# Row chains of a two-layer trunk: the norm weight's product beside the sum of squares, one operation behind the root; the second down projection's last rows, and the last store, by column halves

## Chip, cores and metric

The kernel runs on one core of one Trainium2 chip. The metric is the device time of one execution in microseconds (us), the median of several runs. The engines named below are PE (TensorE, matrix products), ACT (ScalarE), DVE (VectorE), POOL (GpSimd) and SP (SyncE, which here only issues loads). Each engine works through its own list of instructions in order; a value made on one engine is waited for on another by a semaphore. DMAs are issued by SP (loads) and by ACT (stores and a few loads).

## The reference

1024 rows of 1024 numbers pass two layers. In each, a mixer (layer 0: a gated short convolution, layer 1: attention with low-rank queries, keys and values) and an MLP with a squared ReLU (inner width 4096) work on the normalised rows, and their result is normalised again, weighted and added to the stream:

```python
def rmsnorm(x, g):
    xf = x.astype(jnp.float32)
    y = xf * lax.rsqrt(jnp.mean(xf * xf, axis=-1, keepdims=True) + NORM_EPS)
    return (y * g.astype(jnp.float32)).astype(x.dtype)
...
        x = x + g_m[:, None, :] * rmsnorm(y, norm_g[l, 1])
        h = modulate(rmsnorm(x, norm_g[l, 2]), sh_f, sc_f)
        y = squared_relu_mlp(h, mlp_up_w[l], mlp_down_w[l])
        x = x + g_f[:, None, :] * rmsnorm(y, norm_g[l, 3])
    return x
```

The two lines `x = x + g * rmsnorm(y, ...)`, four in all, are the row chains that the change touches. The conditioning `g` and the norm weight are one row of 1024 numbers, held in all 128 partitions as `gmb`; the root's factor differs from row to row.

## The kernel before

**Products.** Each fp32 operand is split into a high part, which ACT copies, and a low part, which DVE subtracts (`split_w`, L158). A product is three matmuls of 128x512 (`mm`, L154): low by high, high by low, high by high. The MLPs work in column and row halves with seven products in place of eight (`first_pairs`, `down_pairs`).

**Row chain.** The rows stand in eight tiles `ys[t]` of 128x1024. `Seam.tile` (L318) does for tile t: `add()`, which adds the last part of the product from PSUM to `y` (DVE, L829 of `down` with 1024 columns or L694 of `down_pairs` with 512); `back()`, the DVE half of steps begun earlier; the squares of `y` with their row sum and the root on ACT (L271, L273); `flush()` of the tile before; for t >= 5 two `front` steps; the reciprocal (L278) and y times root times `gmb` in one operation (L327, DVE); the sum with the stream's rows `xr` (L328, DVE); the store of `xr` to DRAM, issued by ACT (L329); the squares and root of `xr`. `flush` (L311) scales `xr` by its own root into `y`, which is then ready to be turned.

**Steps.** The next product needs the rows turned: its operands have the 1024 columns in partitions. Step k (eight for each half of four tiles) turns four 128x128 blocks on PE (L373, L433) and scales and shifts them on ACT (L374, L436); that is its `front`. Its `back` is the split on DVE: L384/L385 in `first_pairs`' operands, and the low part L442 alone where ACT writes the high part itself.

**The four seams.** Two are at the end of `down` (convolution's output, attention's output): for each of eight tiles 24 matmuls go into one of two PSUM tiles `big`, and `seam.tile` follows. The eight steps of the first half are done between tiles 5 to 7 and in `first_pairs` behind them. There `first(0)`, `first(1)`, `second(0)` are the first products; after `second(0)` a fourth block of weights, `late` (L594, an `ad` tile with the tag "acc", one buffer), is split. The other two seams are those of `down_pairs`: tiles 0 to 3 are finished while it still multiplies, tiles 4 to 7 in the loop at its end, 24 matmuls each. In layer 0 the first half's steps run in that loop, and behind it come `first_latents` (L571: three row blocks m, each over k = 0 to 7, so that block m = 0 needs step k's high part and then its low part) and, in block m = 2, the second half's steps, which need tile 7's `flush`. In layer 1 nothing comes behind: the store of tile 7 to the output is the end.

**Order.** `pinned()` keeps the order in which the program is written on all engines but SP; elsewhere, and on SP, a scheduler orders by priority and by when buffers come free. `down_pairs` loads the rows `xr` of tiles 0 to 5 ahead (`early`), by turns into a tile with the tag "xr" and into the "acc" tile.

## Time and profile before

| | us |
|---|---|
| median of 3 runs | 2160.37 (2159.45 to 2161.99) |
| the profiled execution | 2159.2 |
| its span, first to last instruction or transfer | 2157.4 |
| PE busy | 2062.0 (96%) |
| DVE busy | 1541.2 (71%) |
| ACT busy | 1084.3 (50%) |
| first seam: adds of tiles 0 to 7 (L829) | 345.9 to 388.8 |
| second seam's last four tiles: adds (L694) | 1019.1 to 1039.4 |
| third seam: adds (L829) | 1469.1 to 1513.2 |
| last seam's last four tiles: adds (L694) | 2132.3 to 2149.3 |

The granted clock of PE is a mean of 0.991 over the span. In a timeline a row has the start, the duration, the engine, the line, the operation, what it writes and reads with shapes, how many instructions were joined, and in brackets the idle time ahead and what ended it. A row of waits has the total, the number and the longest of the waits of one line for another.

### The profile page before, as it was taken

To read this page: it belongs to the slowest core of one execution; us is meant where nothing else is said; L and a number is where in the kernel's file an instruction comes from. 1 tells how busy PE (TensorE), PEld (TensorE's weight loads), DVE (VectorE), ACT (ScalarE), POOL (GpSimd) and SP (SyncE) were. 2 spreads that over 40 slices of the span, in tenths; PEclk is the share of its full clock that TensorE was granted. 3 is DMA by queue.
4 is the path that set the end of the run, shared out by engine and by line. 5 is a ranking of instruction groups with operands and counts; after the bars stand their busy time and mean duration, and the time that the engine had idled before them with its cause. 6 is when DMAs were issued, how large, how long until landed. Compare 5 with 4: busy or idle time off the path is not lost.

```text
span 2157.4 us, 25064 instructions
## 1 busy us (share of the span) xinstructions
PE 2062.0 (96%) x9438; PEld 1688.2 (78%) x9438; DVE 1541.2 (71%) x2087; ACT 1084.3 (50%) x1533; POOL 5.3 (0%) x13
## 2 busy tenths in 40 slices
PE   4999999989999999999899999999899999999998
PEld 3788878768888788888677788887678888788886
DVE  6877876876665669977688887756875665566576
ACT  4533353745554444455665565555744444544443
POOL 0000000000000000000000000000000000000000
PEclk9999999999999999999999999999999999999999
DMA  7444464254553889656223331143254653774355
GB/s 223 121 138 147 137 205 133 88 184 161 182 181 139 280 292 322 208 166 211 69 70 120 97 96 35 59 135 138 71 185 150 215 180 134 266 252 158 98 175 167
DMA packets 251023, 344.47 MB, mean 160 GB/s; under 512 B 19253, under 2 KB 142482, under 8 KB 250902
## 3 DMA queue, kind: packets, MB, share of 16 engines
q1 hardware_dynamic: 208408, 252.50, 37.4%
q10 hardware_dynamic: 42494, 90.38, 11.3%
q8 instruction: 74, 1.21, 0.2%
q14 instruction: 47, 0.39, 0.1%
HBM read 258.94 MB, written 83.89 MB: 159 GB/s over the span
## 4 chain that ended last, share of the span: by engine, by line
PE 77%; DVE 11%; ACT 6%; DMA 3%; issue 2%; ACTq 0%; SPq 0%; DVEq 0%
PE one L156 42%; PE mm L156 20%; PE tp L156 7%; PE big L156 3%; PE big L1360 2%; ACT junk L271 2%; DVE y L327 1%; PE tp L1386 1%; DVE raw L328 1%; DMA aw<-in_ada_w_dram 1%; ACT slot L1210 1%; DVE av L909 1%; PE tp L433 1%; DVE ring L160 1%; DVE acc L186 1%
## 5 line engine op out<-in xcount | busy, mean ns | idle before, releaser
L156 PE MATMUL one<-slot,uphi 128*128 128x512 f32 x1224 | 377.8, 389 | 0.0
L156 PEld LDWEIGHTS one<-slot,uphi 128*128 128x128 f32 x1224 | 230.4, 188 | 48.3 <-issue 0.5
L156 PE MATMUL one<-ring,ring 128*128 128x512 f32 x1152 | 262.9, 389 | 2.3 <-DVE ring L160 2.3
L160 DVE TENSOR_TENSOR uplo<-raw,uphi 128x1024 fp32r<-128x1024 f32 x127 | 153.3, 1222 | 143.1 <-ACT uphi L159 143.1
L156 PEld LDWEIGHTS one<-ring,ring 128*128 128x128 f32 x1152 | 215.9, 188 | 48.3 <-ACT ring L159 3.1
L156 PE MATMUL one<-slot,uplo 128*128 128x512 f32 x612 | 240.7, 393 | 8.2 <-DVE y L528 3.8
L160 DVE TENSOR_TENSOR ring<-raw,ring 128x1024 fp32r<-128x1024 f32 x144 | 174.3, 1220 | 55.6 <-ACT ring L159 55.3
L159 ACT ACTIVATE ring<-raw 128x1024 fp32r<-128x1024 f32 x144 | 149.5, 1052 | 106.6 <-DMA raw<-ha 61.6
L159 ACT ACTIVATE uphi<-raw 128x1024 fp32r<-128x1024 f32 x127 | 134.7, 1061 | 118.6 <-PE one L156 82.3
L156 PE MATMUL mm<-ring,ring 128*128 128x512 f32 x768 | 185.0, 390 | 1.6 <-DVE ring L160 1.6
L156 PE MATMUL tp<-ring,ring 128*128 128x512 f32 x768 | 183.9, 389 | 0.0
L159 ACT ACTIVATE ring<-w 128x1024 fp32r<-128x1024 f32 x80 | 84.8, 1060 | 178.7 <-PE tp L156 102.7
L156 PEld LDWEIGHTS mm<-ring,ring 128*128 128x128 f32 x768 | 143.7, 188 | 32.1 <-DVE ring L160 2.5
L156 PEld LDWEIGHTS tp<-ring,ring 128*128 128x128 f32 x768 | 144.1, 188 | 29.9
L160 DVE TENSOR_TENSOR ring<-w,ring 128x1024 fp32r<-128x1024 f32 x80 | 97.8, 1222 | 81.1 <-ACT ring L159 81.1
L156 PEld LDWEIGHTS one<-slot,uplo 128*128 128x128 f32 x612 | 115.2, 188 | 35.8 <-DVE y L528 5.5
L186 DVE SCALAR_TENSOR_TENSOR acc<-raw,csil,acc 128x1024 f32<-128x1024 f32 x88 | 112.5, 1278 | 22.8 <-DMA raw<-in_ada_w_dram 18.0
L526 ACT ACTIVATE y<-one 128x512 f32<-128x512 f32 x66 | 39.0, 591 | 159.6 <-PE one L156 118.5
L156 PE MATMUL mm<-slot,uphi 128*128 128x512 f32 x344 | 109.2, 399 | 9.6 <-DVE slot L398 9.4
L156 PE MATMUL one<-slot,s 128*128 128x512 f32 x468 | 112.9, 390 | 1.1 <-DVE s L160 1.1
L156 PEld LDWEIGHTS one<-slot,s 128*128 128x128 f32 x468 | 87.6, 188 | 20.6 <-DVE s L160 2.4
L156 PE MATMUL one<-q,uphi 128*128 128x512 f32 x328 | 101.9, 392 | 0.0
(267 smaller groups left out, 3614.4 us busy)
## 6 DMA issues: line engine op xcount, KB each, us to landing
ha<-y ACTq DMA_DIRECT2D x224, 256.0 KB, 4.0
raw<-ha SPq DMA_DIRECT2D x112, 512.0 KB, 4.0
raw<-in_ada_w_dram SPq DMA_DIRECT2D x80, 512.0 KB, 4.3
raw<-in_mlp_up_w_dram SPq DMA_DIRECT2D x70, 512.0 KB, 4.5
w<-in_mlp_down_w_dram SPq DMA_DIRECT2D x48, 512.0 KB, 7.0
raw<-in_mlp_down_w_dram SPq DMA_DIRECT2D x32, 512.0 KB, 4.0
raw<-in_conv_in_w_dram SPq DMA_DIRECT2D x18, 512.0 KB, 4.1
xs<-raw ACTq DMA_DIRECT2D x18, 512.0 KB, 2.8
```

Of the source, the lines that this page charges most:

```text
L156: nc.tensor.matmul(out_, lhs[a], rhs[b], start=first and i == 0, stop=last and i == 2, skip_group_check=more)
L159: nc.scalar.activation(hi, src, AF.Copy)
L160: nc.vector.tensor_tensor(lo, src, hi.bitcast(F32), op=ALU.subtract)
L186: nc.vector.scalar_tensor_tensor(acc, raw, s, acc, op0=ALU.mult, op1=ALU.add)
L271: nc.scalar.activation(junk, src, AF.Square, accum_out=ss)
L327: nc.vector.scalar_tensor_tensor(y, y, rroot(ss), self.gmb, op0=ALU.mult, op1=ALU.mult)
L328: nc.vector.tensor_tensor(xr, xr, y, op=ALU.add)
L433: nc.tensor.transpose(p_[:, t * P:(t + 1) * P], ys[half * 4 + t][:, k * P:(k + 1) * P], ident)
L526: nc.scalar.activation(dst, x_, AF.Copy)
L909: nc.vector.scalar_tensor_tensor(acc, raw[:, i, :], csil[:, i:i + 1], acc, op0=ALU.mult, op1=ALU.add)
L1210: nc.scalar.activation(y[32 * i:32 * i + 32, :], p_[32 * j:32 * j + 32, :], AF.Copy, scale=scale)
L1360: nc.tensor.matmul(o_, a, m_, start=j == 0, stop=j == 4)
```

## The change

It does six things.

1. In seams 1 and 3 for all tiles, and in `down_pairs` for tiles 5 to 7 (`seam.beside`), the product with the norm weight, `yg = y * gmb`, is an operation of its own on DVE, which needs no root, into the "acc" tile. Behind the root one operation is left, `xr = yg * root + xr`.
2. The store of `xr` is issued after the squares and the root of `xr`, and `back()` stands at the end of the tile.
3. In tiles 5 to 7 of `down_pairs` (`part`) the second column half, which needs no add any more, is squared and weighted ahead of the add; only the first half's squares follow the add, with the other sum as the root's bias.
4. The last tile's last operation and its store go by column halves, the second half's store by SP.
5. Tile 5's `xr` in `down_pairs` is no longer loaded ahead into the "acc" tile.
6. `late` shares the "acc" buffer with `yg`, and so is loaded behind the last `yg`.

```diff
-    def squares(nx, src):
+    def squares(nx, src, more=None):
...
-        nc.scalar.activation(rt, ss, AF.Sqrt, bias=eps_d)
+        nc.scalar.activation(rt, ss, AF.Sqrt, bias=eps_d if more is None else more)
...
-        def tile(self, t, add, steps):
+        def tile(self, t, add, steps, held=False, part=False):
...
+            beside = add is not None and t >= self.beside
+            part = part and beside
+            yg = ad.tile([P, D], F32, tag="acc", name=nm("yg"), bufs=1) if beside else None
+
+            def gained(cols):
+                nc.vector.tensor_tensor(yg[:, cols], y[:, cols], self.gmb[:, cols], op=ALU.mult)
+
             with pinned():
+                if part:
+                    some = small()
+                    junk = self.nx.tile([P, D], BF16, tag="junk", name=nm("junk"), bufs=1)
+                    nc.scalar.activation(junk[:, HALF:], y[:, HALF:], AF.Square, accum_out=some)
+                    nc.vector.tensor_tensor(some, some, eps_d, op=ALU.add)
+                    gained(slice(HALF, D))
                 if add:
                     add()
-                self.back()
-                ss = squares(self.nx, y)
+                if beside:
+                    gained(slice(0, HALF if part else D))
+                else:
+                    self.back()
+                if part:
+                    ss = squares(self.nx, y[:, :HALF], some)
+                else:
+                    ss = squares(self.nx, y)
                 self.flush()
                 if t >= 5:
                     self.front(steps, 2)
-                nc.vector.scalar_tensor_tensor(y, y, rroot(ss), self.gmb, op0=ALU.mult, op1=ALU.mult)
-                nc.vector.tensor_tensor(xr, xr, y, op=ALU.add)
-                nc.scalar.dma_start(self.xdst[t * P:(t + 1) * P, :], xr)
+                rs = rroot(ss)
+                if not beside:
+                    nc.vector.scalar_tensor_tensor(y, y, rs, self.gmb, op0=ALU.mult, op1=ALU.mult)
+                    nc.vector.tensor_tensor(xr, xr, y, op=ALU.add)
+                elif self.last and t == NT - 1:
+                    for n, queue in enumerate((nc.scalar, nc.sync)):
+                        cols = slice(n * HALF, (n + 1) * HALF)
+                        nc.vector.scalar_tensor_tensor(xr[:, cols], yg[:, cols], rs, xr[:, cols], op0=ALU.mult, op1=ALU.add)
+                        queue.dma_start(self.xdst[t * P:(t + 1) * P, cols], xr[:, cols])
+                    return
+                else:
+                    nc.vector.scalar_tensor_tensor(xr, yg, rs, xr, op0=ALU.mult, op1=ALU.add)
                 if not self.last:
-                    self.rest = (y, xr, squares(self.nx, xr))
+                    self.rest = (y, xr, None, t) if held else (y, xr, squares(self.nx, xr), None)
+                if not held:
+                    nc.scalar.dma_start(self.xdst[t * P:(t + 1) * P, :], xr)
+                if beside:
+                    self.back()
...
-                    early(i // 2)
+                    if i < 10:
+                        early(i // 2)
...
-            seam.ahead = 4
+            seam.ahead, seam.beside = 4, 5
...
-                    seam.tile(4 + t, lambda: done(t, banks_[t]), [])
+                    seam.tile(4 + t, lambda: done(t, banks_[t]), [], False, True)
```

`held` is false everywhere. Inside `tile`, the lines after the change are 36 higher than before (L442 becomes L478, L694 becomes L730, L829 becomes L866).

First place: DVE in the first seam, around the add of tile 6 (`y_2274`; `raw_2772` and then `raw_2775` are the stream's rows of tile 5, `slot_2260` the operand that the steps fill). Before:

```order
L328 TENSOR_TENSOR raw_2772<-raw_2772,y_2273 128x1024
L829 TENSOR_TENSOR y_2274<-y_2274,big_2897 128x1024
L384 CAST slot_2260<-q_2279 128x512
L385 TENSOR_TENSOR slot_2260<-q_2279,slot_2260 128x512
L384 CAST slot_2260<-q_2280 128x512
L385 TENSOR_TENSOR slot_2260<-q_2280,slot_2260 128x512
L278 RECIPROCAL small_2932<-small_2895 128x1
L278 RECIPROCAL small_2947<-small_2930 128x1
L327 SCALAR_TENSOR_TENSOR y_2274<-y_2274,small_2947,gmb_1086 128x1024
L328 TENSOR_TENSOR raw_2818<-raw_2818,y_2274 128x1024
```

After the change, in the same place:

```order
L361 SCALAR_TENSOR_TENSOR raw_2775<-yg_2871,small_2894,raw_2775 128x1024
L420 CAST slot_2260<-q_2279 128x512
L421 TENSOR_TENSOR slot_2260<-q_2279,slot_2260 128x512
L420 CAST slot_2260<-q_2280 128x512
L421 TENSOR_TENSOR slot_2260<-q_2280,slot_2260 128x512
L866 TENSOR_TENSOR y_2274<-y_2274,big_2907 128x1024
L328 TENSOR_TENSOR yg_2932<-y_2274,gmb_1086 128x1024
L278 RECIPROCAL small_2940<-small_2900 128x1
L278 RECIPROCAL small_2955<-small_2938 128x1
L361 SCALAR_TENSOR_TENSOR raw_2822<-yg_2932,small_2955,raw_2822 128x1024
```

The four rows of the two steps moved from behind tile 6's add to ahead of it, the second of the two long rows behind the root is gone, and the product with `gmb` stands between the add and the reciprocals.

Second place: DVE in `down_pairs` of layer 0, tile 5 (`y_5371`, later `y_5379`) and the low part of step 6 (`h_1013_7203` from `tt_7536`, later `h_1021_7211` from `tt_7544`), from the end of tile 4 on. Before:

```order
L328 TENSOR_TENSOR xr_7240<-xr_7240,y_5370 128x1024
L694 TENSOR_TENSOR y_5371<-y_5371,mm_6855 128x512
L442 TENSOR_TENSOR h_1013_7203<-tt_7536,h_1012_7202 128x512
L278 RECIPROCAL small_7558<-small_7529 128x1
L278 RECIPROCAL small_7561<-small_7556 128x1
L327 SCALAR_TENSOR_TENSOR y_5371<-y_5371,small_7561,gmb_4317 128x1024
L328 TENSOR_TENSOR xr_7326<-xr_7326,y_5371 128x1024
```

After the change:

```order
L353 TENSOR_TENSOR xr_7248<-xr_7248,y_5378 128x1024
L335 TENSOR_TENSOR small_7560<-small_7560,eps_d 128x1
L328 TENSOR_TENSOR yg_7559<-y_5379,gmb_4325 128x512
L730 TENSOR_TENSOR y_5379<-y_5379,mm_6863 128x512
L328 TENSOR_TENSOR yg_7559<-y_5379,gmb_4325 128x512
L278 RECIPROCAL small_7572<-small_7536 128x1
L278 RECIPROCAL small_7575<-small_7570 128x1
L361 SCALAR_TENSOR_TENSOR raw_7517<-yg_7559,small_7575,raw_7517 128x1024
L478 TENSOR_TENSOR h_1021_7211<-tt_7544,h_1020_7210 128x512
```

The low part of step 6 moved from the row behind tile 5's add to behind its last operation, and the 128x1 sum L335, which needs ACT's squares of the second half, now stands ahead of the add. The low part of step 7 stands likewise behind tile 6's last operation. The same rows of ACT, from tile 4's root on, before:

```order
L329 DMA xs_104<-xr_7240 128x1024
L271 ACTIVATE junk_7526,small_7527<-xr_7240 128x1024
L273 ACTIVATE small_7529<-small_7527,eps_d 128x1
L436 ACTIVATE h_1012_7202<-one_7531,v_6810,v_6806 128x512
L436 ACTIVATE tt_7536<-one_7531,v_6810,v_6806 128x512
L271 ACTIVATE junk_7553,small_7554<-y_5371 128x1024
L273 ACTIVATE small_7556<-small_7554,eps_d 128x1
L311 ACTIVATE y_5370<-xr_7240,small_7558 128x1024
```

After the change:

```order
L271 ACTIVATE junk_7533,small_7534<-xr_7248 128x1024
L273 ACTIVATE small_7536<-small_7534,eps_d 128x1
L365 DMA xs_104<-xr_7248 128x1024
L472 ACTIVATE h_1020_7210<-one_7539,v_6818,v_6814 128x512
L472 ACTIVATE tt_7544<-one_7539,v_6818,v_6814 128x512
L334 ACTIVATE junk_7561,small_7560<-y_5379 128x512
L271 ACTIVATE junk_7567,small_7568<-y_5379 128x512
L273 ACTIVATE small_7570<-small_7568,small_7560 128x1
L311 ACTIVATE y_5378<-xr_7248,small_7572 128x1024
```

The whole squares of tile 5 became two of half the columns, and the first of them (L334) stands behind the store of tile 4.

Third place: SP in the first seam, between the loads of the stream's last rows and the next weights (`w_3041` is `late`, `acc_4327` a row of biases for the conditioning). After the change:

```order
L296 DMA raw_2869<-in_x_dram 128x1024
L114 DMA raw_3043<-in_mlp_up_w_dram 128x8x128
L114 DMA raw_3045<-in_mlp_up_w_dram 128x8x128
L114 DMA w_3041<-in_mlp_up_w_dram 128x8x128
L114 DMA acc_4327<-in_ada_b_dram 1x1024
L114 DMA raw_3382<-in_mlp_up_w_dram 128x8x128
```

Before, `late` stood 21 rows further up, ahead of most of the output projection's weights:

```order
L114 DMA raw_2438<-in_conv_out_w_dram 128x1024
L114 DMA raw_2442<-hd_116 128x1024
L114 DMA w_3029<-in_mlp_up_w_dram 128x8x128
L114 DMA raw_2558<-in_conv_out_w_dram 128x1024
L114 DMA raw_2562<-hd_117 128x1024
```

It moved past the loads of all eight tiles' rows, and now waits for tile 7's last operation, since it shares the buffer with `yg`. In the third seam it moved in the same way. On PE the transposes of the steps around tiles 6 and 7 of seams 1 and 3 are grouped otherwise between the matmuls; in `down_pairs` and at the end PE's order is the same.

10 lines of the change are left out of this document (6 added, 4 removed).

## The prediction

> **What bounds the kernel now.** I read the page first, for the engine that sets the pace.
>
> ```profile
> span 2157.4 us, 25064 instructions
> PE 77%; DVE 11%; ACT 6%; DMA 3%; issue 2%; ACTq 0%; SPq 0%; DVEq 0%
> ```
>
> The second line is the chain that ended last: 77% of the span is PE's own work, and DVE and ACT appear where PE stands still for them. The change touches no matmul, so it can only move the stretches in which PE waits, the matmuls that run slowly after a wait, and the tail behind the last matmul. The waits of PE come next, by who is waited for.
>
> ```profile
> PE tp L433 <- ACT y L311: 5.8, 2, 5.2
> PE tp L373 <- ACT q L374: 4.9, 4, 2.3
> ```
>
> Both belong to the seams: 4.9 us in four waits for the scaled transposes of seams 1 and 3, and 5.8 us for the normalised last rows of seam 2. The timeline of the end of seam 1 shows what these waits are made of.
>
> ```profile
> 381.50 1.22 DVE L829 TENSOR_TENSOR y<-y,big 128x1024 f32<-128x1024 f32 x1
> ...
> 383.38 1.04 ACT L271 ACTIVATE junk<-y 128x1024 bf16<-128x1024 f32 x1
> ...
> 384.55 0.30 ACT L273 ACTIVATE small<-small,eps_d 128x1 f32<-128x1 f32 x1
> ...
> 385.08 1.28 DVE L327 SCALAR_TENSOR_TENSOR y<-y,small,gmb 128x1024 f32<-128x1024 f32 x1
> ...
> 385.34 0.48 PE L156 MATMUL big<-slot,slot 128*128 128x512 f32 x1
> ...
> 386.40 1.23 DVE L328 TENSOR_TENSOR raw<-raw,y 128x1024 f32<-128x1024 f32 x1
> 386.82 1.33 PE L373 MATMUL tp<-cs,y 128*128 128x128 f32 x8 [1.01 <-ACT q L374]
> 387.54 1.21 DVE L829 TENSOR_TENSOR y<-y,big 128x1024 f32<-128x1024 f32 x1
> ...
> 390.99 1.15 ACT L311 ACTIVATE y<-raw,small 128x1024 f32<-128x1024 f32 x1
> ...
> 392.05 1.43 ACT L374 ACTIVATE q<-tp,v,v 128x512 f32<-128x512 f32 x2
> ...
> 392.86 1.78 PE L373 MATMUL tp<-cs,y 128*128 128x128 f32 x8 [1.19 <-ACT q L374]
> ...
> 401.58 1.05 ACT L159 ACTIVATE uphi<-w 128x1024 fp32r<-128x1024 f32 x1
> ```
>
> PE has finished tile 7's matmuls at 385.8, but its add (L829) starts only at 387.54: the chain lags PE. From that add on everything is serial: squares, root, L311, then the scaled transposes at 392.05, for which PE waits. The clock pays once more:
>
> ```profile
> 380.00:393.00 13.00, 10.57 (x51) 7.60 (x50) 12.69 (x20) 11.25 (x20) 0.00 (x0) 1.00 0.49 161
> 393.00:397.00 4.00, 4.00 (x15) 3.31 (x15) 2.99 (x6) 3.38 (x7) 0.00 (x0) 0.57 0.33 131
> 1048.70:1052.00 3.30, 3.30 (x11) 2.72 (x12) 1.12 (x2) 1.48 (x2) 0.00 (x0) 0.52 0.02 5
> ```
>
> The columns are the stretch, its length, busy time of PE, weight loads, DVE, ACT and POOL, the granted clock and the DMAs. In 380 to 393 DVE is busy for 12.69 of 13 us. In 393 to 397 PE gets 0.57 of its clock, so 4.0 x 0.43 = 1.7 us of its work is lost; behind the long wait of seam 2 it is 3.3 x 0.48 = 1.6 us.
>
> **The change part by part. Seam 1.** L327 and L328 behind the root (1.28 + 1.23) become one operation; I price it by L327, which has two tensors and a column too, at 1.28. The product `yg` costs as much as L328 (1.23) but runs on DVE while ACT squares (1.04 and more). So one L328 leaves the cycle: two adds of before lie 6.04 us apart (381.50 and 387.54), and 6.04 - 1.23 is 4.8. PE needs 5.44 for a tile's 24 matmuls (the adds at the very end, shown below, follow PE: 2148.64 - 2137.77 is two tiles), so PE becomes the pace, and the lag vanishes up to tile 5. For tiles 6 and 7 the steps' splits fill DVE again, as the 12.69 of 13 shows. Written out engine by engine in the new order, the queues give tile 7's add at 386.4, 1.15 earlier. Its squares start when the add ends, at 387.6; 1.4 for squares and root on ACT (383.38 to the end of 384.55's row is 1.47) and 1.06 of L311 (390.99 to 392.05) put the scaled transposes at 390.1 instead of 392.05, so **-2.0**. PE still waits there, some 1.1 us by the same sum, but the wait of 1.01 at 386.82 goes since steps 2 and 3 are turned earlier. With one short wait instead of two I take the slow stretch as gone: **-1.3** of the 1.7, since PE would lose part of it to the same chain anyway. Together -3.3, or -2.0 if the clock drops as before.
>
> The store behind the squares costs nothing: ACT had to issue it in the same cycle before. `back()` at the tile's end costs nothing in this seam, for the casts wait for ACT's L374 in either place.
>
> **Seam 3** has the same code and a worse lag:
>
> ```profile
> 1508.44 0.48 PE L156 MATMUL big<-slot,slot 128*128 128x512 f32 x1
> 1511.93 1.22 DVE L829 TENSOR_TENSOR y<-y,big 128x1024 f32<-128x1024 f32 x1
> ...
> 1516.44 1.43 ACT L374 ACTIVATE q<-tp,v,v 128x512 f32<-128x512 f32 x2
> ```
>
> PE is done at 1508.9, the add comes 3.0 later. Half a microsecond of DVE work stays between them, so the add moves to 1509.5 and the transposes' scaling from 1516.4 to 1513.2. That is 3.2; with 0.2 for a clock that PE now has back sooner I take **-3.4**, or -2.1 if the slow clock comes behind the wait.
>
> **Seam 2** is where the change can lose.
>
> ```profile
> 1022.83 1.22 DVE L328 TENSOR_TENSOR xr<-xr,y 128x1024 f32<-128x1024 f32 x1
> ...
> 1027.31 0.69 DVE L442 TENSOR_TENSOR h<-tt,h 128x512 fp32r<-128x512 f32 x1 [2.65 <-ACT tt L436]
> ...
> 1034.03 0.50 PE L156 MATMUL big<-h,uplo 128*128 128x512 f32 x1 [1.36 <-ACT h L436]
> ...
> 1034.68 0.69 DVE L442 TENSOR_TENSOR h<-tt,h 128x512 fp32r<-128x512 f32 x1 [2.65 <-ACT tt L436]
> ...
> 1035.42 0.73 PE L156 MATMUL big<-h,uphi 128*128 128x512 f32 x2 [0.90 <-DVE h L442]
> ...
> 1044.28 0.63 ACT L1194 ACTIVATE sq<-lat 128x512 f32<-128x512 f32 x1
> ...
> 1047.46 1.14 ACT L311 ACTIVATE y<-raw,small 128x1024 f32<-128x1024 f32 x1
> ...
> 1048.65 0.48 PE L433 MATMUL tp<-cs,y 128*128 128x128 f32 x1 [5.19 <-ACT y L311]
> ```
>
> L442 is the low part that `first_latents` needs for steps 6 and 7; PE waits for step 7's already. It now stands behind tile 6's last operation. ACT's squares of half a tile I take at 0.72: L1194 squares 512 columns in 0.63 without the row sum's reading; the ends are 0.63 and the 1.17 of a whole tile (383.38 to 384.55). L335 on 128x1 I take at 0.16, between nothing and the 0.30 of the 128x1 root. Then per tile: ACT (squares and root of `xr` 1.4, store 0.34, the step's two scalings 1.43, L334 0.72), DVE (L335 0.16, half of `yg` 0.69, add 0.68), ACT (half squares 0.72, root 0.3), DVE (reciprocal 0.2, last operation 1.28): 7.9 by the durations, about 7.7 where neighbours on an engine overlap; before, the two L442 rows lie 7.4 apart. Starting from tile 4's end at 1024.05 tile 5 ends at 1031.8 and tile 6 at 1039.5. Step 6's low part moves from 1027.31 to 1031.8, just when PE reaches it; step 7's from 1034.68 to 1039.5. PE's wait of 0.90 before 1035.42 grows to about 5.3: it resumes near 1040.3. That costs little, for PE waits again later, 5.19 us, for tile 7's L311. That one is what counts, and it moves from 1047.46 to about 1049.0 by the same cycle: **+1.5**. Against it stands the clock: the long wait comes earlier, its slow matmuls then run inside time that is waited out anyway, and the wait ahead of 1048.65 shrinks to some 1.7, so that the 1.6 lost after it may go. From -0.1 to +1.8, I take **+0.6**; with half squares at the whole price 0.45 more for each of two in three tiles, 2.7, so +3.3.
>
> A rule of the Trainium skill bears on this ("TensorE: Matmul & The Clock Gate", section "What's actually happening"): the clock halves after an idle window of about 3.4 us and returns after as long a busy one, in windows that run free. The row above with 0.52 behind a wait of 5.19 agrees; the 0.57 at 393, with no wait over 1.2 us ahead of it, does not. By the rule alone seam 1 would have had no slow stretch before either, and the sum would be 1.3 smaller, -6.1.
>
> **Tail.** The last rows' adds and the last store:
>
> ```profile
> 2136.06 1.23 DVE L328 TENSOR_TENSOR xr<-xr,y 128x1024 f32<-128x1024 f32 x1
> ...
> 2137.77 0.69 DVE L694 TENSOR_TENSOR y<-y,mm 128x512 f32<-128x512 f32 x1 [0.48 <-PE mm L156]
> ...
> 2148.64 0.69 DVE L694 TENSOR_TENSOR y<-y,tp 128x512 f32<-128x512 f32 x1 [0.46 <-PE tp L156]
> 2149.37 1.06 ACT L271 ACTIVATE junk<-y 128x1024 bf16<-128x1024 f32 x1 [3.96 <-DVE y L694]
> ...
> 2153.65 0.34 ACTq L329 DMA_DIRECT2D out_dram<-raw  x1
> ```
>
> Adds follow PE 5.44 apart. The half squares of tile t stand on ACT behind tile t-1's store, and DVE has L335 and half of `yg` ahead of the add. Behind tile 4's end at 2137.28 come the store, L334, L335 and half of `yg` (0.37, 0.72, 0.16, 0.69), so tile 5's add starts at 2139.2, 1.46 late. With add, half squares, root, reciprocal and the last operation (0.69, 0.72, 0.3, 0.2, 1.28, and hops) the new cycle is about 5.26, so the lag falls by 0.18 a tile, and tile 7's add starts at 2149.75, 1.1 late. Then add 0.69, half squares 0.72, root and reciprocal 0.5 end at 2151.7, and the halves (0.69 each, as L442's half operations) issue at 2152.5 on ACT and 2153.1 on SP, the latter 0.55 ahead of 2153.65. The store's landing:
>
> ```profile
> raw<-in_mlp_up_w_dram SPq DMA_DIRECT2D x70, 512.0 KB, 4.5
> ...
> raw<-in_conv_out_w_dram SPq DMA_DIRECT2D x8, 512.0 KB, 7.7
> ...
> out_dram<-raw ACTq DMA_DIRECT2D x2, 512.0 KB, 2.7
> ```
>
> A whole store lands in 2.7. Half of it lies between 1.4, if bytes alone count, and the same 2.7. I take 2.3, nearer to the row: **-0.9** in all, from -0.55 to -1.9. The Trainium skill ("DMA: Bandwidth & Descriptors", section "Issuing engines are not separate DMA queues") says that DMAs from several engines run on the same 16 DMA engines, and a second issuer saves only issue time. By it the halves land no sooner than one store, which is the end of -0.55; no row here has two such stores at once.
>
> **Tile 5's load** no longer runs beside the weights ahead of the last loop.
>
> ```profile
> PE mm L156 <- DVE ring L160: 1.6, 2, 1.0
> ```
>
> These two waits, 1.6 us in all, are just ahead of the last loop, for split weights whose loads run beside that of tile 5's rows. Ends 0 and -1.6; I take **-0.4**, near 0, since the load only moves.
>
> **Sum:** -3.3 - 3.4 + 0.6 - 0.9 - 0.4 = -7.4. The profiled execution took 2159.2 (span 2157.4), so 2151.8 for it; it stands 1.2 under the median of 2160.37, and 2160.37 - 7.4 gives **2153.0**.
>
> **Rivals.** *The clock stays slow.* PE still waits in seams 1 and 3, and the row at 0.57 came after waits of 1 us. Then -2.0 - 2.1, seam 2 at +1.8, the tail at -0.55, nothing for the load: -2.9, **2157.5**. For it: the row itself; against it: the two waits become one.
>
> *The change does less than it says.* PE's chain behind the seams may absorb their gains: what follows `second(0)` waits for loads. Then only the tail is left, **2159.5**. Against it: the first work behind, the split at 401.58, waits for no load and follows PE.
>
> *Slower: `late` arrives late.* It now waits for tile 7's last operation, at 390.6 in seam 1, and its split (401.58, moved to 398.3) is 7.6 us later, with PE's next products behind it. A load of this kind lands in 4.5, the slowest group of such size in 7.7. Each microsecond over 7.6 costs one in both seams: -7.4 + 2 x (L - 7.6) is zero at a landing of 11.3 and passes +4.3 at 13.5, for example **2166** at 14. Against it: DMAs are 0.33 busy then, by the row of 393 to 397.
>
> **How the numbers follow.** A tie is within 0.2%, 4.3 us, about what a measurement of this kernel can tell: faster means below 2156.05. Forecast 0.58, its own range 2150.0 (load -1.6, tail at -1.5, seam 2 at -0.1) to 2156 (one seam with the slow clock, seam 2 at +1.8). Slow clock 0.22, mostly a tie. Absorbed 0.10. Half squares at the whole price 0.03: seam 2 at +3.3 and, in the tail, a cycle of 6.2 that PE no longer hides, some +2.2 in place of -0.9, so -1.6, 2158.8. Slower 0.07. Faster 0.58 + 0.05 = 0.63, the tie 0.30, slower 0.07. The range 2150.0 to 2159 takes in the slow clock and leaves out the rest.
>
> **What would show it.** Seam 1: adds 5.44 apart up to tile 6, the scaled transposes near 390, clock 1.00 behind them. Seam 3: the same near 1513, less 3.3 for the shift. Seam 2: a wait of some 5 us for L478 and a short one for L311. Tail: the last add 1.1 behind the last matmul, stores 0.6 apart. Wrong would be a wait of ACT for `late`, adds still 6 apart, or a long wait for L311 unchanged behind the longer one.

## The result and the profile after

| | us |
|---|---|
| before, median of 4 runs | 2159.91 (2156.31 to 2161.99) |
| after, median of 4 runs | 2148.89 (2147.98 to 2149.11) |
| ratio, 95% interval | 0.9954 (0.9942 to 0.9966) |
| profiled execution after | 2148.73, span 2146.9 |

The kernel is faster by 0.46%, 7 to 12.5 us by the interval. The forecast was 2153.0, with a range from 2150.0 to 2159.0: the direction was right, the time lies 1.1 below the range. The page of after, the same kind of lines as before:

```profile
span 2146.9 us, 25090 instructions
PE 74%; DVE 12%; ACT 6%; DMA 5%; issue 2%; SPq 0%; ACTq 0%; DVEq 0%
```

PE's share of the last chain fell a little and that of the DMAs rose. What the change did is read from the waits of PE in the profile of after:

```profile
PE big L156 <- DVE h L478: 5.6, 2, 5.4
...
PE tp L409 <- ACT q L410: 2.8, 2, 1.4
```

The wait for L311 of 5.2 is gone from the head of the list and a wait of 5.4 for the low part L478 has come, as forecast. The waits of seams 1 and 3 are two instead of four. The timeline of seam 1 after (start, duration, engine, line, operation, operands, count, idle time ahead), which runs 2.2 us earlier than before from the start of the seam on:

```profile
370.89 1.22 DVE L866 TENSOR_TENSOR y<-y,big 128x1024 f32<-128x1024 f32 x1 [1.19 <-PE big L156]
...
377.51 1.22 DVE L866 TENSOR_TENSOR y<-y,big 128x1024 f32<-128x1024 f32 x1
...
384.11 1.22 DVE L866 TENSOR_TENSOR y<-y,big 128x1024 f32<-128x1024 f32 x1
...
387.78 1.43 ACT L410 ACTIVATE q<-tp,v,v 128x512 f32<-128x512 f32 x2
388.41 0.37 SPq L114 DMA_DIRECT2D w<-in_mlp_up_w_dram  x1
...
388.59 1.33 PE L409 MATMUL tp<-cs,y 128*128 128x128 f32 x8 [1.43 <-ACT q L410]
...
395.91 1.05 ACT L159 ACTIVATE uphi<-w 128x1024 fp32r<-128x1024 f32 x1
```

Up to tile 5 the adds are 5.44 apart and wait for PE; those of tiles 6 and 7, around which the steps' splits fall, are 6.6 apart, where "adds 5.44 apart up to tile 6" was to show it. With 2.2 added, tile 7's add is at 386.3 (forecast 386.4), the scaled transposes at 390.0 (390.1), the split of `late` at 398.1 (398.3). `late` is issued at 388.41 and split 7.5 us later in its turn, between other ACT work: it is not waited for. One wait of 1.43 is left of 1.01 and 1.19, and the windows behind it (PE, weight loads, DVE, ACT, POOL, granted clock, DMA share, GB/s) show a whole clock:

```profile
393.00:397.00 4.00, 4.00 (x19) 3.33 (x18) 1.22 (x5) 2.97 (x4) 0.00 (x0) 1.00 0.02 5
```

Seam 3 after, shifted by 5.9 at its start, has the add at 1509.5 (1509.5) and the scaled transposes at 1513.2 (1513.2):

```profile
1503.59 1.21 DVE L866 TENSOR_TENSOR y<-y,big 128x1024 f32<-128x1024 f32 x1
...
1507.26 1.43 ACT L410 ACTIVATE q<-tp,v,v 128x512 f32<-128x512 f32 x2
...
1508.07 1.33 PE L409 MATMUL tp<-cs,y 128*128 128x128 f32 x8 [1.34 <-ACT q L410]
```

Seam 2 after, 5.0 earlier at its start (tile 4's add at 1014.11, before at 1019.09):

```profile
1034.40 0.68 DVE L478 TENSOR_TENSOR h<-tt,h 128x512 fp32r<-128x512 f32 x1
...
1035.14 1.22 PE L156 MATMUL big<-h,uphi 128*128 128x512 f32 x2 [5.43 <-DVE h L478]
...
1043.43 1.15 ACT L311 ACTIVATE y<-raw,small 128x1024 f32<-128x1024 f32 x1 [0.23 <-DVE small L278]
...
1044.64 0.33 PE L469 MATMUL tp<-cs,y 128*128 128x128 f32 x1 [0.21 <-ACT y L311]
```

With the shift L478 is at 1039.4 (forecast 1039.5), PE resumes at 1040.1 (1040.3), and L311 comes at 1048.4 (1049.0). The low clock now lies behind the first wait, ahead of tile 7's L311, and no longer behind L311, for which PE now waits only 0.21:

```profile
1036.00:1040.00 4.00, 4.00 (x11) 3.12 (x11) 2.29 (x6) 2.43 (x7) 0.00 (x0) 0.55 0.69 238
...
1044.00:1047.00 3.00, 2.79 (x20) 2.19 (x18) 1.15 (x3) 2.97 (x5) 0.00 (x0) 1.00 0.25 96
```

The tail after, and the landing of its stores (the second half's was not recorded):

```profile
2138.62 0.19 ACT L334 ACTIVATION_READ_ACCUMULATOR junk<-y 128x1 f32 x1
...
2139.52 0.68 DVE L730 TENSOR_TENSOR y<-y,tp 128x512 f32<-128x512 f32 x1
...
2142.36 0.34 ACTq L358 DMA_DIRECT2D out_dram<-raw  x1
2143.01 0.34 SPq L358 DMA_DIRECT2D out_dram<-raw  x1
```
```profile
out_dram<-raw ACTq DMA_DIRECT2D x1, 256.0 KB, 2.1
```

PE's last matmul ends at 2138.57, and the add follows 0.95 later (forecast 1.1), held up by L334. Half a store lands in 2.1 (I took 2.3), but the other half, issued last, leaves 3.9 us to the end of the span, as the whole store does (3.75 before).

**One ruler for all runs.** All kernels have the same 9438 matmuls on PE, so the starts of the same matmul (by its number in order of start) can be compared, and the span cut at them. This table, in us, takes matmuls 1100 to 1230 (the output projection's weights), 1475 to 1650 (seam 1), 4300 to 4420 (seam 2), 6640 to 6770 (seam 3), 9300 to the last (the last weights and the loop of tiles 4 to 7), and the last matmul's start to the end of the span.

| profile | 1100-1230 | seam 1 | seam 2 | seam 3 | 9300-last | tail |
|---|---|---|---|---|---|---|
| before | 33.43 | 41.03 | 35.07 | 30.44 | 33.31 | 9.19 |
| before, again (e11) | 34.54 | 40.00 | 35.16 | 31.69 | 32.69 | 9.31 |
| after | 31.75 | 37.58 | 34.52 | 27.01 | 32.32 | 8.76 |
| after, again (e5) | 31.77 | 37.56 | 34.51 | 27.00 | 33.07 | 8.67 |
| e1 block moved | 32.31 | 40.06 | 35.99 | 30.50 | 35.29 | 9.41 |
| e2 pairs only | 34.21 | 38.82 | 34.51 | 29.36 | 33.03 | 8.18 |
| e3 seams 1, 3 only | 32.48 | 37.57 | 33.61 | 27.02 | 32.91 | 9.10 |
| e4 half early | 32.06 | 37.59 | 30.72 | 27.02 | 32.27 | 7.29 |
| e6 half and low part early | 31.93 | 37.59 | 27.81 | 27.01 | 32.51 | 7.29 |
| e7 whole store | 32.48 | 37.59 | 34.49 | 27.01 | 32.51 | 8.59 |
| e8 tile 5 early | 34.23 | 37.59 | 34.54 | 27.01 | 38.05 | 7.11 |
| e9 no half split | 33.00 | 37.58 | 31.20 | 27.02 | 32.62 | 7.48 |
| e10 order only | 32.11 | 43.06 | 35.07 | 33.82 | 32.66 | 9.11 |
| e12 tile 5's load dropped | 32.29 | 39.96 | 35.14 | 30.39 | 32.63 | 9.11 |
| e13 splits beside | 32.35 | 39.18 | 34.55 | 28.70 | 32.30 | 8.50 |

From the profile of before to the first of after the columns differ by -1.7, -3.5, -0.6, -3.4, -1.0 and -0.4, which is all of the -10.5 between the spans. The runs were to tell which of these are the change's and which are scatter.

### The profile page after: what moved, and what is told of

Read it like the earlier page. It is cut to its first block, busy times and chain, and to the rows that moved or that the text cites. A ratio compares the mean times of both kernels' runs of the same rounds, so it can differ in the third digit from the quotient of the medians.

```text
span 2146.9 us, 25090 instructions
## 1 busy us (share of the span) xinstructions
PE 2057.8 (96%) x9438; PEld 1685.5 (79%) x9438; DVE 1542.4 (72%) x2100; ACT 1085.8 (51%) x1545; POOL 5.3 (0%) x13
## 4 chain that ended last, share of the span: by engine, by line
PE 74%; DVE 12%; ACT 6%; DMA 5%; issue 2%; SPq 0%; ACTq 0%; DVEq 0%
PE one L156 39%; PE mm L156 19%; PE tp L156 6%; PE big L156 5%; PE big L1397 2%; DMA raw<-ha 2%; DVE ring L160 1%; PE tp L1423 1%; ACT junk L271 1%; ACT slot L1247 1%; DMA w<-in_mlp_down_w_dram 1%; ACT ring L159 1%; DMA aw<-in_ada_w_dram 1%; DVE acc L186 1%; DVE uplo L160 1%
```

## The experiments

Medians are each beside runs of the kernel before on the same chip; the ratio is to those.

**e1, the fourth weight block's move alone.** My first theory for the surplus of the result was the move of `late`, which I had priced only as a risk: before, it was issued at 297.31, just ahead of two loads of the output projection, and PE waited there.

```diff
+                rt_ = rroot(ss)
...
+                if add and t == NT - 1 and self.ahead == 3:
+                    hold = ad.tile([P, D], F32, tag="acc", name=nm("hold"), bufs=1)
+                    nc.vector.tensor_copy(hold[:, :1], rt_)
```

> The kernel before with one thing of the change: the fourth weight block is loaded behind tile 7 of seams 1 and 3 instead of ahead of the output projection's weights (a one-column copy into its buffer at tile 7 holds it back). Row chains as before. Theory (the move itself gains): PE's wait for L831 near 309 us falls from 2.6 to about 1.0, the two loads that took 7.5 and 7.8 us land in about 5, and the time is 2.0 to 2.5 us below before. Rival (the 2 us are run-to-run scatter of loads): within 0.7 us of before. Rival on record (the block arrives late): a wait of ACT for it near 398 us, slower than before.

Measured: 2158.40 (12 runs), before 2157.73 (23 runs), ratio 1.0002 (0.9993 to 1.0011). A gain of 2.0 to 2.5 us is excluded, and so is a loss of over 2.4. The wait near 309 is 1.5 in its profile, but it is no longer only the move that makes it small: in e10 and e12, where `late` is loaded early as before, it is 1.3 and 1.4. The rows in which PE waits, first of before, then of e12:

```profile
309.24 3.03 PE L156 MATMUL big<-slot,slot 128*128 128x512 f32 x12 [2.62 <-ACT y L831]
```
```profile
307.25 8.55 PE L156 MATMUL big<-slot,slot 128*128 128x512 f32 x36 [1.43 <-ACT y L832]
```

So this wait scatters by itself: 1.3 to 2.6 in the five profiles with `late` loaded early, 1.0 to 2.3 in the ten with it moved. By the interval, what is left for the move is at most about 1.5.

**e2 and e3, the change in halves.** e2 leaves seams 1 and 3 as before, e3 the two `down_pairs` loops.

```diff
-            self.rest, self.backs, self.xr, self.ahead, self.beside = None, [], {}, 3, 0
+            self.rest, self.backs, self.xr, self.ahead, self.beside = None, [], {}, 3, NT
```
```diff
-            seam.ahead, seam.beside = 4, 5
+            seam.ahead, seam.beside = 4, NT
```

> The kernel after with the row chains of seams 1 and 3 as before (and so the fourth weight block loaded early again); tiles 5 to 7 of both down_pairs loops and the last store as changed, tile 5's early load dropped. Theory: seam 2 gives 0.3, the tail 0.5, the dropped load 0.3, so 1 us below before (0.5 to 1.5), and the wait of 2.6 near 309 us is back. Rival (scatter of loads gave the 2 us): 3 us below.

> The kernel after with both down_pairs loops as before (no product beside, whole squares, whole store), tile 5's early load dropped; seams 1 and 3 as changed. Theory: 2.2 for the block's move, 3.6 and 3.3 for the two chains, 0.3 for the load: 9 to 9.5 us below before. In seam 2 the wait of 5.2 us for L311 is back and the low clock behind it; PE's wait for the low part is 0.9. Rival (seam 2's and the tail's part is worth more than the ledger of matmul starts says): 7 us or less below before.

Measured: e2 2153.76 (11 runs), ratio 0.9977 (0.9968 to 0.9986), 4.0 below before by medians and 5.0 by the ratio; e3 2148.89 (5 runs), ratio 0.9955 (0.9944 to 0.9967), 8.8 and 9.7; both beside 2157.73. e3's number came as expected, but by luck: its theory counted 2.2 for the block's move, which e1 excludes, and nothing for seam 2, which is 1.7 shorter than in the old kernels (33.61, mean 35.3). It also shows that product and column halves in `down_pairs` add nothing to the whole that these runs can tell: without them the time is 2148.89, with them 2149.05 (after, over 9 runs). e2 gave more than its theory, and the table shows where: seams 1 and 3, at 38.82 and 29.36, are 1 us shorter than in before and e11, e1 or e12, though I had called them left as before. They are not: without the product beside, `tile` still issues the store behind the squares and root of `xr`. The timeline of e2 between two adds:

```profile
356.36 1.22 DVE L866 TENSOR_TENSOR y<-y,big 128x1024 f32<-128x1024 f32 x1
356.48 1.06 ACT L271 ACTIVATE junk<-raw 128x1024 bf16<-128x1024 f32 x1 [1.76 <-DVE raw L353]
...
357.67 0.33 ACTq L365 DMA_DIRECT2D xs<-raw  x1
...
362.21 1.21 DVE L866 TENSOR_TENSOR y<-y,big 128x1024 f32<-128x1024 f32 x1
```

ACT's squares begin 0.12 after the add's start instead of 0.49 (381.50 and 381.99 in before), and the store's 0.37 falls partly into the root's time, so adds are 5.85 apart instead of 6.03: 0.18 for each of five tiles and 0.06 for tile 7, 1.0 us a seam. Seam 2 in e3 has the store's new place too, and so counts as neither old nor new; that the store is what shortens it is not shown by itself. So the two runs share a part, and their gains add to more than the whole's.

**e4, the early half's squares ahead of the previous store.** In the tiles with column halves, L334 moved from behind tile t's store to behind tile t's root and flush, for tile t+1.

```diff
...
+            def early_half(i):
+                if i < NT:
+                    self.some[i] = small()
+                    junk = self.nx.tile([P, D], BF16, tag="junk", name=nm("junk"), bufs=1)
+                    nc.scalar.activation(junk[:, HALF:], self.ys[i][:, HALF:], AF.Square, accum_out=self.some[i])
...
                 self.flush()
+                if ahead_half:
+                    early_half(t + 1)
```

> The kernel after with the early half's squares of tile t+1 issued behind tile t's root and flush, so ahead of tile t's store and of the squares of the stream's rows. Theory (these squares sit in the tile to tile cycle of down_pairs, which is bound by the row chain): the cycle falls from 7.7 to about 5.7 us in seam 2, the low part of step 7 comes about 4 us earlier, PE's wait of 5.4 us falls to about 1.5 and the low clock behind it goes; in the tail the last add follows PE by 0.2 instead of 0.95. Together 4 to 7 us below the kernel after, 14 to 17 below before. Rival (tile 7's L311 sets the end of seam 2 anyway): only the tail's 0.8 and up to 1 in seam 2, 10.5 to 12 below before.

Measured: 2142.64 (5 runs), ratio 0.9932 (0.9919 to 0.9944), 15.1 below before and 6.4 below after's 2149.05 (9 runs). Seam 2 is 3.8 shorter and the tail 1.4; the add follows PE at once. The sum came as expected, its theory only in part: the wait for the low part fell from 5.4 to 3.0 and not to 1.5, since the low part still stood behind the tile's last operation, and the half clock behind the wait stayed (6.83 us from 1030.68). The row of e4:

```profile
1031.28 1.22 PE L156 MATMUL big<-h,uphi 128*128 128x512 f32 x2 [3.01 <-DVE h L484]
```

**e5, after again.** No edit.

> The kernel after, unchanged, for a larger sample of both kernels. Theory (the profile of before was one with many low-clock windows, and the median of its first runs stood high): before again at 2157 to 2158, after at 2148.5 to 2149.5, so 8.5 to 9 us below before. Rival (the first comparison was right): 10 to 11.5 below before. In the profile of after no low-clock window near 393 (seam 1) or near 1512 (seam 3), whatever its phase.

Measured: 2149.20 (5 runs, 2146.68 to 2149.43), before 2157.02 (13 runs), ratio 0.9960 (0.9947 to 0.9972), 7.8 below before. The theory holds, a little low, though the interval of these runs alone (6.0 to 11.4) leaves room for the rival. Of all 67 runs of before in this study the median is 2157.53 (2153.2 to 2164.1, standard deviation 2.3), of the 9 of after 2149.05 (standard deviation 0.9). The change is worth 8.5 us by medians and 9.3 by means (2157.94 and 2148.68), and the first runs of before stood 2.4 to 2.8 above the kernel's level.

**e6, the low part early too.** e4 with `back()` behind the product in the tiles with halves, ahead of the reciprocals.

```diff
-                else:
+                if part or not beside:
                     self.back()
...
-                if beside:
+                if beside and not part:
                     self.back()
```

> The kernel with the early half's squares ahead of the previous tile's store (as in the run before), and in down_pairs the steps' low part on DVE beside the squares, ahead of the tile's last operation, instead of behind it. Theory (the low part of step 7 sets PE's wait): it comes 2.3 us earlier, the wait of 3.0 falls below 1, no low clock behind it, and then tile 7's L311 is what PE waits for: 1.5 to 3 us below the run with the half's squares alone, 16 to 18 below before. Rival (the low part delays the tile's own reciprocal and last operation, so that L311 comes later by what PE gains): within 0.7 of that run.

Measured: 2140.79 (5 runs), ratio 0.9923 (0.9910 to 0.9935), the best kernel of the study: 8.3 below after and 1.9 below e4 (their intervals overlap; the seam tells them apart). Seam 2 is another 2.9 shorter. The low part is waited for 0.68 and L311 is what PE now waits for, with no low clock between, in the timeline of e6:

```profile
1029.70 0.73 PE L156 MATMUL big<-h,uphi 128*128 128x512 f32 x2 [0.68 <-DVE h L484]
...
1039.00 0.33 PE L475 MATMUL tp<-cs,y 128*128 128x128 f32 x1 [2.10 <-ACT y L311]
```

**e7, the last store whole.**

```diff
-                elif self.last and t == NT - 1:
+                elif False:
```

> The kernel after with tile 7's last operation and store whole, one operation of 1024 columns and one DMA by ACT. Theory (two issuers save only issue time, and the second half's DMA is issued later than a whole one would be): the store is issued 0.1 us earlier than the second half now is, and the stretch from the last matmul to the end, 8.8 in the profile of after, stays within 0.3. Rival (half a store lands sooner): that stretch grows by 0.5 or more.

Measured in one run, 2149.90: the tail is 8.59 against 8.76 and 8.67, so beside these two profiles the halves gain nothing. The whole store is issued 3.37 after the add, the second half 3.49 after it (2143.01 - 2139.52). One run does not settle it, though: from the last store's issue to the end of the span, the seven profiles with a whole store take 3.67 to 3.98 (mean 3.79), the eight with halves 3.18 to 3.94 (mean 3.49), of which after and e5, at 3.94 and 3.85, are the longest. The timeline of e7:

```profile
2140.85 0.68 DVE L730 TENSOR_TENSOR y<-y,tp 128x512 f32<-128x512 f32 x1
...
2144.22 0.34 ACTq L365 DMA_DIRECT2D out_dram<-raw  x1
```

**e8, tile 5's rows early again**, into a raw tile, since "acc" is `yg`'s.

```diff
                     if i < 10:
                         early(i // 2)
+                    else:
+                        seam.load(5, raw_tile())
```

> The kernel after with tile 5's rows loaded ahead in down_pairs again (into a buffer of the ring of raw tiles, so one of four is held meanwhile). Theory (that load runs beside weights for which PE waits ahead of the last loop): PE's waits for split weights near 2120 grow from 1.0 to 1.6 or more, 0.3 to 1.5 us above the kernel after. Rival (the load is hidden, and the shorter stretch there in the profile of after is scatter): within 0.3 of the kernel after.

Measured: 2153.06 (9 runs), ratio 0.9976 (0.9966 to 0.9986), 4.0 above after. But this is probably the buffer more than the load: with one of four raw tiles held, PE waits for a split 3.63 us, which no kernel with the load into "acc" shows (1.0 at most). The row of e8:

```profile
2126.71 8.71 PE L156 MATMUL mm<-ring,ring 128*128 128x512 f32 x30 [3.63 <-DVE ring L160]
```

It does not tell what the load itself costs. Its tail of 7.11 fits: PE's late matmuls give the row chain time to catch up.

**e9, whole squares and product in `down_pairs`.**

```diff
-                    seam.tile(4 + t, lambda: done(t, banks_[t]), [], False, True)
+                    seam.tile(4 + t, lambda: done(t, banks_[t]), [], False, False)
```

> The kernel after with the squares and the product of down_pairs' tiles 5 to 7 whole and behind the add (the product beside the squares stays, one operation behind the root stays). Theory (the early half's squares sit behind the previous tile's store and hold up the add, so that the column halves cost more than they save): the cycle in seam 2 falls from 7.7 to about 6.1 us, PE's wait for step 7's low part from 5.4 to about 2, in the tail the last add follows PE directly; 2.5 to 4 us below the kernel after. Rival (the halves shorten the chain behind the add, as they are written to): in seam 2 no gain, the tail 0.4 longer, 0.3 to 1 above the kernel after.

Measured: 2146.83 (5 runs), before 2156.96 (15 runs), ratio 0.9947 (0.9935 to 0.9960): 2.2 below after by medians, with seam 2 3.3 and the tail 1.2 shorter by the table. The wait for the low part is 3.6, not 2, but its fall from 5.4 and the table are clear: the column halves, where the change puts them, cost more than they save. The last add, in its profile, follows PE at once, and the stores are issued 3.2 and 3.9 behind it instead of 2.8 and 3.5, which the lag of 0.95 outweighed.

**e10, the order alone.** Before, with the splits at the tile's end and the store behind the squares in seams 1 and 3.

```diff
-                self.back()
+                late_back = add is not None and self.ahead == 3
+                if not late_back:
+                    self.back()
...
+                if late_back:
+                    nc.scalar.dma_start(self.xdst[t * P:(t + 1) * P, :], xr)
+                    self.back()
```

> The kernel before with only the order of the change in seams 1 and 3: the steps' splits at the tile's end, ahead of the next add, and the store behind the stream's squares; the two operations behind the root stay. Theory (the shorter chain gives the gain, the order costs and gains nothing): within 0.7 us of before; adds still 6.0 apart, and from the first add of seam 1 to the first products behind it 38.8 to 41 us as before, 29.4 to 30.5 in seam 3. Rival (splits ahead of the add are what frees the first products): 2 to 6 us below before, those two stretches at 37.6 and 27.0.

Measured: 2163.40 (10 runs), ratio 1.0033 (1.0024 to 1.0043): 6.4 slower by medians, against theory and rival alike. Seams 1 and 3 are 3 us longer each, though the store's new place alone, as e2 shows, makes them 1.0 shorter: the splits' place costs some 4 (4.2 and 4.5 beside e2, with low-clock stretches at 392.29, 1511.87 and 1518.69 in this profile). The adds of tiles 6 and 7 are now 7.5 apart, not 6.0, and PE waits 3.48, in the timeline of e10:

```profile
379.74 1.21 DVE L835 TENSOR_TENSOR y<-y,big 128x1024 f32<-128x1024 f32 x1
...
387.29 1.21 DVE L835 TENSOR_TENSOR y<-y,big 128x1024 f32<-128x1024 f32 x1
...
391.77 1.78 PE L379 MATMUL tp<-cs,y 128*128 128x128 f32 x8 [3.48 <-ACT q L380]
```

Before, the splits (2.2 us) lay beside ACT's squares, between add and reciprocal; ahead of the add they lengthen the serial chain.

**e11, before again.** No edit, one run.

> The kernel before, unchanged, for one more profile. Theory (its scatter comes from low-clock windows that fall or don't fall on the short waits of seams 1 and 3, of the loop ahead of the end and of others): seam 1 between 38.8 and 41.0, seam 3 between 29.4 and 30.5, according to windows of 3.4 us in them; the stretch with the output projection's loads near 309 at 33.4 to 34.2, above every run in which the fourth weight block was moved and no low window fell there (31.7 to 32.5). Rival (the stretches are stable and the first profile was typical): 41.0, 30.4 and 33.4 within 0.2.

Measured, 2159.99: 34.54, 40.00 and 31.69, where the first profile had 33.43, 41.03 and 30.44. The stretches scatter by 1 us, and low-clock windows go with it: in this profile 3.41 us near 309 and 3.41 near 1517, but none near 393, where the first had one and is 1.0 longer. Seam 3 fell outside what I had expected, 1.2 above.

**e12, tile 5's load dropped from before.**

```diff
-                    early(i // 2)
+                    if i < 10:
+                        early(i // 2)
```

> The kernel before without tile 5's early load in down_pairs (its rows are then loaded by SP with those of tiles 6 and 7). Theory (the load runs beside weights that PE waits for): the two waits for split weights ahead of the last loop, 1.6 to 2.0 us in profiles of before, fall to 1.0 to 1.4. Rival (no effect): they stay at 1.6 or more. The total is not expected to tell this from scatter.

Measured in one run, 2156.72: one wait of 1.00 is left ahead of the last loop. But e11, with the load, has one of 1.00 too. So this is not settled: the waits are 1.6, 2.0, 1.0 and 1.0 in four profiles with the load, 0.9 to 1.4 in ten without.

**e13, the splits in their old place in the changed kernel.**

```diff
-                else:
+                if not part:
                     self.back()
...
-                if beside:
+                if part:
                     self.back()
```

> The kernel after with the steps' splits of seams 1 and 3 in their place of before, behind the add (here behind add and product, ahead of the reciprocals), instead of at the tile's end. Theory now (with the order alone both seams grew by 3 us: DVE has no room in tiles 6 and 7, so whatever stands ahead of the add or ahead of the last operation lengthens one of two paths; with the product beside, product and splits together outlast ACT's squares, and the last operation waits for them): the add of tile 7 starts 0.4 earlier, but the last operation 1.4 later and the scaled transposes with it; the stretches of seams 1 and 3 grow from 37.6 and 27.0 to about 39.2 and 28.6, 3 us above the kernel after. Rival (splits ahead of the add hold the change back as they did in the kernel before): the stretches fall below 36.5 and 26, 2 to 4 us below the kernel after.

Measured: 2151.69 (9 runs), before 2157.80 (12 runs), ratio 0.9972 (0.9961 to 0.9982), 2.6 above after; the stretches are 39.18 and 28.70, as worked out ahead. Its timeline:

```profile
382.87 1.29 DVE L361 SCALAR_TENSOR_TENSOR raw<-yg,small,raw 128x1024 f32<-128x1024 f32 x1
...
384.46 1.22 DVE L866 TENSOR_TENSOR y<-y,big 128x1024 f32<-128x1024 f32 x1 [0.30 <-PE big L156]
...
390.23 1.43 ACT L410 ACTIVATE q<-tp,v,v 128x512 f32<-128x512 f32 x2
```

Product and splits now outlast ACT's squares, and the last operation waits for them. The splits' place that cost some 4 us a seam in the old chain is worth 1.6 in the new one.

## Why the forecast was wrong, and where it was right

**The step that failed is the last line of the sum:** "it stands 1.2 under the median of 2160.37, and 2160.37 - 7.4 gives 2153.0". It took the median of three runs as the kernel's level and gave it no width. Over 67 runs that level is 2157.53, 2.8 lower, with single runs from 2153 to 2164. From there -7.4 gives 2150.1, and after lies at 2149.05 over 9 runs. So of the 4.1 us between 2153.0 and 2148.89, 2.8 are the base and about 1.1 the terms; 0.2 is after's own scatter. My first explanation, the moved weight block, took a scattering wait of one profile for an effect; e1 excludes the size that I gave it, and e10 and e12 show the wait short without the move. The range failed with the base: it added the bounds of the terms and none for where the kernel before stands. With a scatter of 2.3 between runs, a median of three is uncertain by some 1.6 (an estimate from that scatter), so 2.8 too high may be chance alone; whether more stood behind it, the record does not show. By means (2157.94 and 2148.68) the base is 2.4 of it and the terms 1.9. The ends were mis-added as well: load -1.6, tail -1.5 and seam 2 at -0.1 give 2150.5, not 2150.0, and one seam with the slow clock and seam 2 at +1.8 give 2155.5, not 2156.

**Seam 1, -3.3:** the schedule came as worked out (adds 5.44 apart up to tile 5, tile 7's chain to 0.2 us), and e3 keeps the gain without the pairs. But the product is only part of it: e2, without it, keeps 1.4 of the 2.7 here and 1.4 of the 3.8 in seam 3, by the store's new place. Against one profile it was -3.5; against the four of the old chain (41.03, 40.00, 40.06, 39.96, mean 40.3) it is -2.7, for the low clock that I took as always there falls there only in some executions, and costs 1.0 where it does (41.03 against 40.0), not the 1.3 that I took.

**Seam 3, -3.4:** 30.8 is the mean of the four old ones (30.44, 31.69, 30.50, 30.39), 27.0 after: -3.8.

**"The store behind the squares costs nothing":** wrong: it gains 1.0 us in a seam of the old chain by the spacing of the adds (e2). In the new one PE sets the pace there, and it can't be seen apart.

**"`back()` at the tile's end costs nothing in this seam":** wrong as a reason. In the old chain it costs some 4 us a seam (e10 beside e2), in the new one it gains 1.6 (e13). What the term of -3.3 contains is therefore not the product alone but product and order together. With the store in its new place, one profile each gives for seam 1 and seam 3: 38.8 and 29.4 with neither (e2), 39.2 and 28.7 with the product alone (e13), 43.1 and 33.8 with the splits' place alone (e10), 37.6 and 27.0 with both (after).

**Seam 2, +0.6:** the mechanism held step by step, with L478 and PE's restart to 0.2 us and the low clock moved ahead of L311. L311 came 0.6 earlier than worked out, and no low clock follows it: 34.5 against a mean of 35.3 in five old ones (before, e1, e10, e11, e12), -0.8. The price of the half squares was right: 0.63 and 0.19 of reading, on ACT 0.72 in all. What I forecast as a loss in waiting is real: e4 and e9 take it away and gain 3.3 to 3.8 in this seam.

**Tail, -0.9:** -0.5 (9.2 in the same five, 8.7 after). The lag of the add was right (0.95 for 1.1). The landing did not come in after: its last half ends 3.9 behind its issue, no sooner than a whole store, where 0.4 sooner was forecast; over all profiles with halves it is 0.3 sooner on average (e7). By what the Trainium skill says ("DMA: Bandwidth & Descriptors", section "Issuing engines are not separate DMA queues"), a second issuer saves issue time only; e7 beside after agrees, 8.6 with a whole store and 8.7 with halves. But e2, e4, e6, e8 and e9, whose last half ends 3.2 to 3.4 behind its issue, do not, so this stays open.

**Tile 5's load, -0.4:** open. The column from 9300 on has a mean of 33.5 in four profiles with the load and 32.8 in five without (after, e5, e2, e3, e12), and both overlap. The difference hangs on one profile, e1 (35.29), which has a low-clock stretch at 2131.0; without it the mean with the load is 32.9.

**The rivals.** The slow clock did not stay: none near 393 or 1512 in any profile of the new chain. `late` arriving late did not happen. Nor were the gains absorbed: at matmul 9300 the profile of after is 9.0 ahead of that of before (2105.87 and 2114.91), 9.3 ahead behind seam 3.

Summed over the means, -2.7 - 3.8 - 0.8 - 0.5 - 0.7 is -8.5, beside 8.5 by all runs. That they agree to 0.1 is partly chance: each mean is of two to five profiles, and the sum leaves out the table's first column, which by the same means (33.3 in the five, 31.8 in after and e5) would add -1.6. A part of that for the moved block is neither shown nor excluded.

## To carry over

Take the level of a kernel from as many runs as its own scatter needs before adding terms to it, and let the range hold that scatter; a wait in one profile is a sample too. When a product is moved beside another engine's work, put down for that engine what else stands in the same gap: here product and splits did not both fit beside the squares, and beyond the store's new place only the two moves together gained. Work that needs nothing of a serial chain belongs ahead of the chain's own store and squares on its engine: L334 and the low part, moved so, gave as much again as the change.

## What the hardware showed

The granted clock drops in stretches of 3.41 us or a multiple (6.83, 10.24), in the trace's record of the clock; only the last drop of each profile, which the end cuts off, has another length. In each of the fifteen profiles all drops start whole multiples of 3.413 us apart: in before at 38.13, at 393.12 (104 of them later) and at 1512.69 (432). The step of 3.41 ahead of a drop held little work: in before PE was busy for 2.00 us from 389.71 to 393.12, and in no profile was it busy for more than 2.03 ahead of a drop, though some steps with less had none behind them (down to 1.5). So behind short waits the same code drops in one execution and not in another, by how the waits fall into the steps. Before had 0.57 in 393 to 397 behind a wait of 1.19; e11, the same kernel, has the same wait, in a step with 2.12 of work, and no drop behind it. Its wait of PE, that step and the stretch behind the wait:

```profile
393.62 1.33 PE L373 MATMUL tp<-cs,y 128*128 128x128 f32 x8 [1.19 <-ACT q L374]
```
```profile
391.00:394.41 3.41, 2.12 (x10) 1.00 (x9) 3.34 (x6) 3.09 (x6) 0.00 (x0) 1.00 0.10 40
393.50:397.50 4.00, 3.87 (x20) 3.16 (x21) 2.99 (x6) 3.39 (x8) 0.00 (x0) 1.00 0.33 131
```

The Trainium skill's windows that run free and are about 3.4 us long ("TensorE: Matmul & The Clock Gate", section "What's actually happening") fit these lengths and that chance; that a wholly idle window is needed does not fit, since PE was busy for 2.00 of the 3.41 us ahead of the drop at 393.12. Nor does the drop behind the prediction's row at 0.52 fit it: that one began at 1045.06, inside the wait of 5.19, and PE was busy for 1.19 of the 3.41 ahead of it. A drop of 3.41 us costs PE up to 1.7 (half of it). It goes with part of the scatter between runs (2.3 us): of the 63 runs of before whose clock the experiments list, the 9 with a mean granted clock of 0.988 or 0.989 took 2161.2 on average, the 14 with 0.992 or more 2156.4. The kernel after, in whose profiles no drop falls into seams 1 and 3, scatters by 0.9.
